# Second parts of weights kept in DRAM: own buffers for the work done ahead, and one unread matmul inside a norm's last sums

## The chip, the cores and the metric

The kernel runs on one core of a Trainium2 chip. The metric is the device time of one execution in microseconds. TensorE (PE) multiplies, VectorE (DVE) and ScalarE (ACT) do elementwise work, GpSimd (POOL) helps them, and SyncE (SP) issues most DMA transfers.

## The reference

One inference step of a decoder with two layers, for 256 prompt tokens and 8 x 4 sample tokens, T = 288 in all, width 2048. Each sub-layer stands between two RMS norms. The even layer mixes tokens by causal pooling and retention, the odd layer by a gating MLP and a convolution of 31 taps over 1024 channels; each layer ends with a dense MLP of 8192 hidden units.

```python
def _rms(x, g):
    y = xf * lax.rsqrt(jnp.mean(xf * xf, axis=-1, keepdims=True) + EPS)
...
for each layer:
    x = x + _rms(mixer(_rms(x, g0) @ w_in) @ w_out, g1)
    x = x + _rms(square(relu(_rms(x, g2) @ w_up)) @ w_down, g3)
```

## The kernel before

**Tiles and passes.** Activations lie transposed, 16 tiles of 128 channels by 288 tokens. Weights are float32; the kernel splits each weight into a hi part in TensorE's rounded float32 type (`whi`, a copy on ScalarE) and the rest (`wlo` = raw - whi, on VectorE), and the activations likewise (`xhi`, `xlo`, or `hidhi`, `hidlo`). Each product is three passes: hi by hi, lo by hi, hi by lo.

**Subs and groups.** The unit of weights is a sub: 256 rows by 512 columns, 512 KB, 24 matmuls. A group (`Grp`) is the subs that fill the same four accumulators of 128 outputs; behind its last sub `evac` empties them. There are 720 subs in a fixed order: the even layer's input projection and mixers; its output projection; the first feed-forward network ("ffn0": four quarters q, each with four up and four down groups of 8 subs, here up0q0g1 or dn0q2g3); the odd layer's input projection (8 groups of 8 subs: ga0, ga1, ga2, v0, v1, ga3, u0, u1); its output projection (two halves of four groups of 4 subs, here oo00 to oo13); the second feed-forward network.

**The weight path.** For each place of the list `feed`, SP loads the raw weights into one of 4 buffers (`emit_dma`), ScalarE makes whi (`emit_hi`) and VectorE wlo (`emit_lo`). The pairs lie in a ring of 3 plus, in some stages, `more_ring(n)` further slots. `run` is the loop over subs; at the start of each it issues pending writes (`put_out`), feeds up to two places ahead (`some`), and then issues the sub's matmuls (`emit_mm`, L604). A load stands in SP's order behind the wait for its buffer.

**Jobs.** In ffn0 the feed holds 60 extra places of kind "job", at subs 1 and 5 of a group (`JOBS`). A job splits a sub of a later stage and writes both parts to DRAM (`hik`, `lok`, L534). When that sub's turn comes its kind is "kept": its parts are loaded from there (L517, two transfers) and not split. Kept are all of ga0, every other sub of the rest of the odd layer, and the first group of the second feed-forward network. A job takes a slot of the ring, as a sub does.

**Norms.** At the end of a sub-layer `last_sums` adds up the squares of the last four tiles on TensorE (L313); `boundary` then issues `keep_warm` (L369, matmuls of ones with a sum that nobody reads), spreads the result (L303) and normalises.

**The convolution** of the odd layer runs in the background of the w_in_odd and w_out_odd subs: some channel tiles on VectorE (`conv_all`, cacc), some on ScalarE and POOL (`conv_slow`, tap), the sample tokens on POOL and VectorE (prod). A tap is issued only when an engine's load, counted in the planner's own costs, is under a cap. `conv_out` ends it with a layer norm (L1347, L313, L303).

All of ScalarE's, VectorE's and POOL's instructions pass one helper, so they all have line L162.

Of the kernel before, what the change touches and what calls it, by code (L numbers as in the profile page):

```python
# [19 lines left out]
T = SEQ + NS  # L20
# [158 lines left out]
def build(tc, ctx, I, O, C):  # L179
# [230 lines left out]

    def last_tiles(src, m):

        if m < OWN:
            add_sq(accs[0], 12 + m, src)
            return
        s = tmp()
        A.activation(out=s, in_=src, func=AF.Square)
        P["own", m] = s
# [3 lines left out]
    def last_sums(i):  # L422

        if i == 0:
            sum_open()
            sum_part(accs[0], first=True)
            sum_part(P.pop(("own", 1)))
        elif i == 1:
            sum_part(P.pop(("own", 2)))
            sum_part(P.pop(("own", 3)), last=True)  # L430

# [42 lines left out]
    RAW, RING = 4, 3  # L474
    JOBS = (1, 5)
    raws, his = {}, {}
# [15 lines left out]
    def emit_dma(p):  # L492
        kind, i = feed[p]
        if kind == "kept":
            return
        g, s = subs[i]
        raw = wp.tile([128, 2, 512], F32, tag="raw", name="raw", bufs=RAW)
        r0, r1 = g.rows[2 * s], g.rows[2 * s + 1]
        assert r1 == r0 + 1 and ORDER[i] == (*g.w, r0, tuple(g.pieces))
        for k in range(0 if p else 2):  # L500
            SP.dma_start(out=raw[:, k, :], in_=I["wt"][i, :, k, :])
        if p:
            SP.dma_start(out=raw, in_=I["wt"][i])
        raws[p] = raw
# [7 lines left out]
    def emit_hi(p):  # L512
        kind, i = feed[p]
        hi, lo = parts[p] = ring_slot()
        if kind == "kept":
            for a, b in zip((hi, lo), kept[i]):
                SP.dma_start(out=f(a), in_=b)  # L517
        else:
            A.activation(out=hi, in_=raws[p], func=AF.Copy)
        if kind != "job":  # L520
            his[i] = hi, lo

    def emit_lo(p):
        kind, i = feed[p]
        hi, lo = parts.pop(p)
        if kind != "kept":
            V.tensor_tensor(out=lo, in0=raws.pop(p), in1=f(hi), op=SUB)
        if kind == "job":
            kept[i] = [dram.tile([128, 2, 512], F32, tag=f"{t}{i}", name=f"{t}k") for t in ("hi", "lo")]
            W["out"] = [(b, a) for a, b in zip((hi, lo), kept[i])]  # L530

# [4 lines left out]
    def plan():  # L536

        todo = []
        where = {}
        at = 0  # L540
        for gi, g in enumerate(groups):
            for s in range(g.nsub):
                subs.append((g, s))
                if g.ahead and g.ahead(s):
                    todo.append(at + s)
            where[gi] = at
            at += g.nsub
        slots = [where[gi] + s for gi, g in enumerate(groups) if g.jobs for s in g.jobs]
        assert len(slots) >= len(todo)
        slots = dict(zip(slots, todo))  # L550
        ahead = set(todo)
        for i in range(len(subs)):
            pos.append(len(feed))
            feed.append(("kept" if i in ahead else "sub", i))
            if i in slots:
                feed.append(("job", slots[i]))
        n = 0
        for kind, i in feed:
            nraw.append(n)
            n += kind != "kept"  # L560
        nraw.append(n)
# [19 lines left out]
    def some(n):  # L581

        return min(W["split"] + n - 1, pos[W["now"]] + RING + W["extra"] - 1)

# [65 lines left out]
    def run():  # L650
# [3 lines left out]
        for i, (g, s) in enumerate(subs):  # L654
# [29 lines left out]
            if last:  # L684
                if g.defer:
                    for m in range(4):
                        if g.keep:
                            g.keep(m, g.ps[m][:, :T])
                        else:
                            A.copy(out=y(m), in_=g.ps[m][:, :T])  # L690
                    def rest(g=g):
                        yield from finish_pre(g.ready)
                        for m in range(0 if g.keep else 4):
                            g.evac(m, y(m))
                        if g.fin:
# [24 lines left out]
    def to_ffn():  # L720
        if E["stack"]:
            E["stack"].close()
            E["stack"] = None
        else:
            Q["stack"].close()
            less_ring()
        more_ring(2)


    def ffn(layer, last):  # L730
        wu, wd = ("w_up", layer), ("w_down", layer)
        for q in range(4):
            for gm in range(4):
                def ev_up(m, ps, gm=gm):
                    k = gm * 4 + m
                    u = W["pool"].tile([128, T], F32, tag="u", name="u", bufs=8)
                    V.scalar_tensor_tensor(out=u, in0=ps, scalar=0.0, in1=rb, op0=ALU.max, op1=MUL)
# [7 lines left out]
                def st_up(q=q, gm=gm):  # L745
                    if gm == 0:
# [4 lines left out]
                                  start=st_up, kouter=first, defer=first, jobs=() if last or first else JOBS,  # L751
                                  ahead=(lambda s: True) if last and first else None))
            for gm in range(4):
                def ev_dn(m, ps, gm=gm, q=q):
# [5 lines left out]
                    if q == 3:  # L760
# [3 lines left out]
                        else:  # L764
                            last_tiles(y(k), m)

                def fin_dn(q=q, gm=gm):
                    if q == 3 and gm == 3:
                        for m in range(4):
# [6 lines left out]
                                  post=to_odd if q == 3 and gm == 1 and not last else None,  # L776
                                  jobs=() if last or (q == 3 and gm == 3) else JOBS))

# [330 lines left out]
    def even():  # L1109
# [35 lines left out]
        for gm in range(4):  # L1145
            def ev_o(m, ps, gm=gm):
# [5 lines left out]
                else:  # L1152
                    last_tiles(ps, m)
                V.tensor_scalar_mul(out=y(k), in0=ps, scalar1=gain(1, 0, k))
# [337 lines left out]
    def odd():  # L1492
# [9 lines left out]
        def ga(j):  # L1502
            def post_ga():
                if j == 1:
                    bg_drain(st_["setup"])
                if j == 0:
                    while "begun" not in Q:
# [8 lines left out]
                              start=odd_open if j == 0 else None, post=post_ga, kouter=j == 0, defer=j == 0,  # L1516
                              ahead=lambda s: j == 0 or s % 2 == 1))

        def vgrp(gm):
            def post_v():  # L1520
                if gm == 1:
# [4 lines left out]
                              lambda m, ps: ev_v_odd(m, ps, gm), start=start_v_odd if gm == 0 else None,  # L1526
                              post=post_v, ahead=lambda s: s % 2 == 1))

        def ugrp(gm):
            def post_u():  # L1530
                if gm == 1:
                    bg_drain(st_["gate"])

                    def tail():
                        while any(c in bgs or c in fills for c in st_["conv"]):
# [6 lines left out]
            groups.append(Grp(w, [(512 * gm, 512)], list(range(KT)), xs, lambda m, ps: ev_u(m, ps, gm),  # L1542
                              start=start_u if gm == 0 else None, post=post_u, ahead=lambda s: s % 2 == 1))

        for fn, i in ((ga, 0), (ga, 1), (ga, 2), (vgrp, 0), (vgrp, 1), (ga, 3), (ugrp, 0), (ugrp, 1)):
            fn(i)
        for half in range(2):
            for gm in range(4):
                def ev_o(m, ps, gm=gm, half=half):
# [5 lines left out]
                    else:  # L1555
# [4 lines left out]
                        else:  # L1560
                            last_tiles(y(k), m)

                def post_o(gm=gm, half=half):
                    if half == 0 and gm == 3:
                        for c in st_["conv"]:
# [12 lines left out]
                                  before={0: hold_ring} if half == 0 and gm == 3 else None,  # L1578
                                  ahead=lambda s: s % 2 == 1))

# [129 lines left out]
```

## Time and profile before

| | |
|---|---|
| median of 3 runs | 2472.33 us (2472.2 to 2473.88) |
| profiled execution | 2476.82 us, span 2475.1 us |
| busy, share of the span | PE 98%, DVE 55%, ACT 44%, POOL 10% |
| granted TensorE clock, mean | 0.988 |
| ffn0 from its first down group to its last sums (548.75 to 1234.19) | 685.44 us |
| odd layer, input projection (1268.30 to 1505.61) | 237.31 us |
| odd layer, output projection and norm (1505.61 to 1640.08) | 134.5 us |

The span runs from the first to the last instruction of the profiled execution, and its time has some microseconds around it. Windows are in microseconds from the start of the span. A busy share of 98% hides that the stages differ; the rows further down are therefore taken by stage. A granted clock of 1.00 is 2.4 GHz, the upper of two levels.

### The profile page before, as it was taken

The page shows a single profiled execution, that of the slowest core. Times are in us where ns is not written, and L with a number is a line of the kernel's source. Part 1 is how long each engine was busy: PE and PEld are TensorE (multiplying, and loading weights), DVE is VectorE, ACT ScalarE, POOL GpSimd, SP SyncE. Part 2 cuts the span into 40 slices and gives each one's busy share as a digit, 9 for nine tenths or more (in the row PEclk, how much of TensorE's full clock was granted, in tenths as well). Part 3 has the DMA queues.
Part 4 walks back from the last instruction along what each step waited for, and adds up shares of the span by engine and source line. Part 5 has one row for each costly group of instructions (what it writes and reads, how often), then busy time and mean ns, then how long its engine had stood idle before and what let it go on. Part 6 is the DMA issues. An engine that isn't in the chain of part 4 may idle for free.

```text
span 2475.1 us, 43388 instructions
## 1 busy us (share of the span) xinstructions
PE 2420.7 (98%) x17976; PEld 2386.2 (96%) x17976; DVE 1360.7 (55%) x1844; ACT 1090.6 (44%) x1567; POOL 251.9 (10%) x293
## 2 busy tenths in 40 slices
PE   9999999999999999999999999899999999999997
PEld 8899999999999999999999999899999999999997
DVE  5665564764455556555546976346434544544453
ACT  5343443554544455455434443435434434433442
POOL 0521111000000000000114750100000000000011
PEclk9999999999999999999999999999999999999998
DMA  7555464588888888888775656455555554545552
GB/s 253 164 185 181 159 206 160 181 280 296 289 289 297 279 295 290 294 288 293 261 254 211 246 200 219 179 196 190 168 164 168 163 169 161 172 162 170 165 166 92
DMA packets 146871, 529.35 MB, mean 214 GB/s; under 512 B 16809, under 2 KB 17849, under 8 KB 146649
## 3 DMA queue, kind: packets, MB, share of 16 engines
q1 hardware_dynamic: 142240, 511.81, 60.4%
q0 software_dynamic: 4288, 14.71, 1.8%
q8 instruction: 140, 2.29, 0.4%
q14 instruction: 59, 0.48, 0.1%
q10 hardware_dynamic: 144, 0.07, 0.0%
HBM read 453.68 MB, written 73.87 MB: 213 GB/s over the span
## 4 chain that ended last, share of the span: by engine, by line
PE 84%; DVE 6%; DMA 4%; ACT 3%; issue 2%; SPq 0%; POOL 0%; DVEq 0%; ACTq 0%; POOLq 0%
PE mm L604 81%; DVE wlo L162 2%; DVE cacc L162 2%; DMA raw<-in_wt 2%; DMA wlo<-lok 1%; ACT whi L162 1%; ACT tmp L162 1%; PE ms L313 1%; DMA lok<-wlo 1%; PE po L995 1%; DVE tmp L162 1%; PE ms L999 0%; DVE conv L162 0%; DVE yo L162 0%; PE ms L303 0%
## 5 line engine op out<-in xcount | busy, mean ns | idle before, releaser
L162 DVE TENSOR_TENSOR wlo<-raw,whi 128x1024 fp32r<-128x1024 f32 (+1 forms) x721 | 886.9, 1240 | 751.1 <-ACT whi L162 737.3
L162 ACT ACTIVATE whi<-raw 128x1024 fp32r<-128x1024 f32 (+1 forms) x721 | 755.1, 1057 | 1011.2 <-PE mm L604 892.1
L604 PE MATMUL mm<-xhi,wlo 128*128 128x288 f32 x3200 | 944.9, 297 | 11.3 <-DVE wlo L162 9.2
L604 PE MATMUL mm<-xhi,whi 128*128 128x288 f32 x3200 | 944.2, 297 | 10.3 <-DVE tmp L162 6.2
L604 PE MATMUL mm<-xlo,whi 128*128 128x288 f32 x3200 | 919.6, 296 | 0.0
L604 PE MATMUL mm<-hidhi,whi 128*128 128x288 f32 x2560 | 754.8, 296 | 6.8 <-ACT whi L162 3.2
L604 PE MATMUL mm<-hidhi,wlo 128*128 128x288 f32 x2560 | 757.6, 297 | 2.5 <-DMA wlo<-lok 1.7
L604 PE MATMUL mm<-hidlo,whi 128*128 128x288 f32 x2560 | 745.2, 296 | 0.0
L604 PEld LDWEIGHTS mm<-xhi,wlo 128*128 128x128 f32 x3200 | 605.4, 189 | 16.0 <-DVE wlo L162 13.2
L604 PEld LDWEIGHTS mm<-xhi,whi 128*128 128x128 f32 x3200 | 605.9, 189 | 13.3 <-issue 6.8
L604 PEld LDWEIGHTS mm<-xlo,whi 128*128 128x128 f32 x3200 | 595.8, 189 | 0.5 <-DVE xlo L162 0.5
L604 PEld LDWEIGHTS mm<-hidhi,whi 128*128 128x128 f32 x2560 | 485.3, 190 | 8.1 <-ACT whi L162 3.4
L604 PEld LDWEIGHTS mm<-hidhi,wlo 128*128 128x128 f32 x2560 | 485.4, 190 | 3.3 <-DMA wlo<-lok 2.1
L604 PEld LDWEIGHTS mm<-hidlo,whi 128*128 128x128 f32 x2560 | 480.3, 189 | 0.0
L162 POOL TENSOR_TENSOR acc<-acc,tmp 128x288 f32<-128x288 f32 x55 | 53.3, 970 | 1657.1 <-ACT tmp L162 1654.3
L162 DVE TENSOR_TENSOR y<-mm,y 128x288 f32<-128x288 f32 x112 | 50.9, 457 | 103.3 <-PE mm L604 103.3
L162 DVE SCALAR_TENSOR_TENSOR u<-mm,rb 128x288 f32<-128x288 f32 x120 | 54.3, 457 | 71.2 <-PE mm L604 71.2
L162 DVE SCALAR_TENSOR_TENSOR cacc<-gx,vecs,cacc 128x256 f32<-128x256 f32 x168 | 68.5, 478 | 0.0
L162 ACT ACTIVATE hidhi<-u 128x288 fp32r<-128x288 f32 x128 | 56.9, 445 | 4.1
L162 ACT ACTIVATE u<-u 128x288 f32<-128x288 f32 x128 | 55.3, 432 | 7.0 <-DVE u L162 6.9
L162 POOL TENSOR_TENSOR conv<-conv,tap 128x256 f32<-128x256 f32 x60 | 53.7, 895 | 13.6 <-ACT tap L162 10.0
L162 DVE TENSOR_TENSOR hidlo<-u,hidhi 128x288 fp32r<-128x288 f32 x128 | 49.7, 450 | 0.0
(180 smaller groups left out, 909.8 us busy)
## 6 DMA issues: line engine op xcount, KB each, us to landing
raw<-in_wt SPq DMA_DIRECT2D x719, 512.0 KB, 4.2
hik<-whi SPq DMA_DIRECT2D x60, 512.0 KB, 6.4
lok<-wlo SPq DMA_DIRECT2D x60, 512.0 KB, 7.1
whi<-hik SPq DMA_DIRECT2D x60, 512.0 KB, 4.4
wlo<-lok SPq DMA_DIRECT2D x60, 512.0 KB, 5.8
s0t<-in_state_ret POOLq DMA_DIRECT2D x24, 256.0 KB, 3.3
out<-s0t POOLq DMA_DIRECT2D x24, 256.0 KB, 3.4
out<-yo SPq DMA_DIRECT2D x8, 288.0 KB, 2.4
```

Source lines behind the costliest of these rows:

```text
L162: return call(*args, **kw)
L313: PE.matmul(P["sums"][:, t:t + 1], lhsT=a[:, c:c + 128], rhs=ones[:, 0:1], start=first and t == 0, stop=last and t == 2)
L604: PE.matmul(ps, lhsT=lhsT[:, k, c], rhs=rhs, start=s == 0 and k == 0 and which == 0, stop=s == g.nsub - 1 and k == 1 and which == 2)
L995: PE.matmul(po[gq:gq + 32, 0:256], lhsT=E["qdm"][:, hh, 32 * (b + i):32 * (b + i + 1)], rhs=s[:, i, :], start=False, stop=b >= 4, tile_pos ...
```

## The change

Jobs no longer use the ring. They have buffers of their own, `jhi` (one) and `jlo` (two), and stand at subs 3, 5 and 7. In ffn0 the ring has 3 + 1 slots in place of 3 + 2, and the tile `u` has 4 buffers there in place of 8. A kept sub has a kind: of "both", hi and lo are stored and loaded, as before (ga0 and the first group of the second feed-forward network); of "lo", only lo is stored, and the raw weights are loaded again so that ScalarE makes hi. "lo" are all subs of ga1 to u1. At the three norms behind ffn0, the odd output projection and the second feed-forward network, one `keep_warm` matmul stands between the sums of the third and of the last tile.

```diff
-    def last_tiles(src, m):
+    def last_tiles(src, m, rest):
+        P["rest"] = rest
...
             sum_part(P.pop(("own", 2)))
+            if P.pop("rest"):
+                keep_warm(1)
             sum_part(P.pop(("own", 3)), last=True)
...
-    JOBS = (1, 5)
+    JOBS = (3, 5, 7)
...
-        if kind == "kept":
+        if kind == "both":
             return
...
-        hi, lo = parts[p] = ring_slot()
-        if kind == "kept":
-            for a, b in zip((hi, lo), kept[i]):
-                SP.dma_start(out=f(a), in_=b)
+        if kind == "job":
+            parts[p] = [W["pool"].tile([128, 2, 512], F32R, tag=t, name=t, bufs=n) for t, n in (("jhi", 1), ("jlo", 2))]
+            A.activation(out=parts[p][0], in_=raws[p], func=AF.Copy)
+            return
+        hi, lo = parts[p] = his[i] = ring_slot()
+        if kind == "both":
+            SP.dma_start(out=f(hi), in_=kept[i][0])
         else:
             A.activation(out=hi, in_=raws[p], func=AF.Copy)
-        if kind != "job":
-            his[i] = hi, lo
+        if kind != "sub":
+            SP.dma_start(out=f(lo), in_=kept[i][-1])
...
         if kind == "job":
-            kept[i] = [dram.tile([128, 2, 512], F32, tag=f"{t}{i}", name=f"{t}k") for t in ("hi", "lo")]
-            W["out"] = [(b, a) for a, b in zip((hi, lo), kept[i])]
+            out = (hi, lo) if feed[pos[i]][0] == "both" else (lo,)
...
-        return min(W["split"] + n - 1, pos[W["now"]] + RING + W["extra"] - 1)
+        return min(W["split"] + n - 1, pos[min(W["now"] + RING + W["extra"], len(subs)) - 1])
...
                         yield from finish_pre(g.ready)
+                        flush()
...
-                                  ahead=(lambda s: True) if last and first else None))
+                                  ahead=(lambda s: "both") if last and first else None))
...
-                                  jobs=() if last or (q == 3 and gm == 3) else JOBS))
+                                  jobs=() if last or (q == 3 and gm > 0) else JOBS))
...
-                              ahead=lambda s: j == 0 or s % 2 == 1))
+                              ahead=lambda s: "both" if j == 0 else "lo"))
...
-                                  ahead=lambda s: s % 2 == 1))
+                                  ahead=lambda s: "lo" if half == 0 and s % 2 else None))
```

In the built order 72 subs are kept, not 80: 16 of "both" and 56 of "lo". The last line's condition is evaluated when `half` is already 1, so no sub of the odd output projection is kept; before, 16 of them were. VectorE's splits go from 721 to 719 (647 wlo and 72 jlo), ScalarE's from 721 to 775, raw loads from 719 to 775, loads of kept parts from 120 to 88, writes from 120 to 88, and TensorE has three matmuls more.

The first place is SP's order in the second and third groups of ffn0. Before, between up0q0g1 and up0q0g2 (raw is a load of weights, hik and lok are writes of a job's parts):

```order
L503 DMA raw_5336<-in_wt 128x1024
L503 DMA raw_5365<-in_wt 128x1024
L503 DMA raw_5374<-in_wt 128x1024
L534 DMA hik_5372<-whi_5367 128x1024
L534 DMA lok_5373<-wlo_5368 128x1024
L503 DMA raw_5406<-in_wt 128x1024
L503 DMA raw_5436<-in_wt 128x1024
L503 DMA raw_5466<-in_wt 128x1024
L503 DMA raw_5495<-in_wt 128x1024
```

In the changed kernel, in up0q0g2 (k0 and k1 are the writes of a job's hi and lo):

```order
L542 DMA k0_5341<-jhi_5332 128x1024
L542 DMA k1_5342<-jlo_5333 128x1024
L506 DMA raw_5376<-in_wt 128x1024
L506 DMA raw_5405<-in_wt 128x1024
L506 DMA raw_5414<-in_wt 128x1024
L542 DMA k0_5411<-jhi_5402 128x1024
L542 DMA k1_5412<-jlo_5403 128x1024
L506 DMA raw_5446<-in_wt 128x1024
```

Within a group there are now three raw loads from one pair of writes to the next, where there were five.

The second place is ScalarE's order at the same point of the program. Before (whi_5367 is a job's, the others are subs'):

```order
L162 ACTIVATE whi_5332<-raw_5186 128x1024
L162 ACTIVATE whi_5362<-raw_5195 128x1024
L162 ACTIVATE whi_5367<-raw_5272 128x1024
L162 ACTIVATE whi_5402<-raw_5294 128x1024
L162 ACTIVATE whi_5432<-raw_5336 128x1024
```

In the changed kernel (jhi is a job's, in the one buffer):

```order
L162 ACTIVATE whi_5294<-raw_5154 128x1024
L162 ACTIVATE jhi_5332<-raw_5163 128x1024
L162 ACTIVATE whi_5337<-raw_5197 128x1024
L162 ACTIVATE whi_5372<-raw_5272 128x1024
L162 ACTIVATE jhi_5402<-raw_5298 128x1024
L162 ACTIVATE whi_5407<-raw_5335 128x1024
```

jhi_5402 writes over jhi_5332, whose write to DRAM is k0_5341 in SP's order above, and whi_5407 of the next sub stands behind it.

The third place is SP's order in the odd layer's input projection, from ga0 on into ga1. Before:

```order
L517 DMA whi_13864<-hik_5942 128x1024
L517 DMA wlo_13865<-lok_5943 128x1024
L503 DMA raw_13898<-in_wt 128x1024
L517 DMA whi_13948<-hik_6072 128x1024
L517 DMA wlo_13949<-lok_6073 128x1024
L503 DMA raw_13956<-in_wt 128x1024
```

In the changed kernel:

```order
L523 DMA whi_13874<-k0_5705 128x1024
L527 DMA wlo_13875<-k1_5706 128x1024
L527 DMA wlo_13905<-k0_5775 128x1024
L506 DMA raw_13908<-in_wt 128x1024
L527 DMA wlo_13959<-k0_5929 128x1024
L506 DMA raw_13962<-in_wt 128x1024
```

Each sub of ga1 and behind now has two transfers and no wlo on VectorE. Two subs had three transfers before, and now have four.

## Rows read from the trace of the kernel before

**Rows 1.** Busy time by stage; behind it granted clock, DMA share, GB/s.
```profile
core 0 of [0], span 2475.1 us
core 0: us, PE busy (x) PEld busy (x) DVE busy (x) ACT busy (x) POOL busy (x), PEclk, DMA share, GB/s
464.75:548.75 84.00, 80.10 (x590) 79.16 (x589) 54.71 (x75) 50.78 (x80) 0.85 (x1) 0.98 0.79 273
548.75:1234.19 685.44, 685.44 (x5186) 685.44 (x5185) 380.47 (x410) 330.48 (x401) 7.55 (x7) 1.00 0.84 288
1234.19:1268.30 34.11, 33.10 (x235) 31.65 (x233) 13.53 (x20) 13.52 (x23) 8.16 (x10) 0.95 0.70 230
1268.30:1505.61 237.31, 222.80 (x1632) 219.44 (x1631) 181.86 (x359) 100.82 (x191) 110.72 (x118) 0.97 0.62 225
1505.61:1627.50 121.89, 114.81 (x800) 112.96 (x801) 44.18 (x81) 47.70 (x90) 10.82 (x14) 0.93 0.60 217
1627.50:1640.08 12.58, 12.06 (x67) 10.80 (x65) 3.55 (x9) 3.81 (x9) 1.41 (x2) 0.73 0.55 205
```

**Rows 2.** Waits of PE in the input projection of the odd layer.
```profile
PE mm L604 <- DVE tmp L162: 6.2, 3, 3.0
PE ms L1439 <- DVE mb L162: 2.9, 1, 2.9
PE mm L604 <- DMA wlo<-lok: 2.0, 2, 1.2
PE mm L604 <- DMA whi<-hik: 1.3, 1, 1.3
```

**Rows 3.** Waits of PE in the output projection of the odd layer.
```profile
PE mm L604 <- ACT whi L162: 3.2, 1, 3.2
PE mm L604 <- DVE tmp L162: 2.1, 1, 2.1
PE mm L604 <- DMA wlo<-lok: 1.7, 2, 1.2
PE mm L604 <- DVE wlo L162: 0.9, 1, 0.9
PE mm L604 <- DMA whi<-hik: 0.5, 1, 0.5
```

**Rows 4.** Timeline of PE after one such wait.
```profile
1355.66 0.37 PE L604 MATMUL mm<-xhi,whi 128*128 128x288 f32 x1 [2.96 <-DVE tmp L162]
...
1356.56 0.44 PE L604 MATMUL mm<-xhi,whi 128*128 128x288 f32 x1
```

**Rows 5.** Groups of VectorE in the input projection of the odd layer.
```profile
L162 DVE TENSOR_TENSOR wlo<-raw,whi 128x1024 fp32r<-128x1024 f32 x29 | 44.1, 1520 | 22.5 <-ACT whi L162 22.5
```

**Rows 6.** Groups on the page; DMA issues on the page, with us to landing.
```profile
L162 DVE TENSOR_TENSOR wlo<-raw,whi 128x1024 fp32r<-128x1024 f32 (+1 forms) x721 | 886.9, 1240 | 751.1 <-ACT whi L162 737.3
L162 ACT ACTIVATE whi<-raw 128x1024 fp32r<-128x1024 f32 (+1 forms) x721 | 755.1, 1057 | 1011.2 <-PE mm L604 892.1
...
hik<-whi SPq DMA_DIRECT2D x60, 512.0 KB, 6.4
```

**Rows 7.** Timelines of POOL and of VectorE about 1346 us.
```profile
1345.09 3.10 POOL L162 TENSOR_TENSOR prod<-gx,vecs 128x992 f32<-128x992 f32 x1
...
1346.15 3.12 DVE L162 TENSOR_TENSOR wlo<-raw,whi 128x1024 fp32r<-128x1024 f32 x1
```

**Rows 8.** Timeline of PE at the norm behind the first feed-forward network.
```profile
1262.93 0.83 PE L313 MATMUL ms<-cg,tmp 128*128 128x1 f32 x6 [0.52 <-ACT tmp L162]
1263.62 1.61 PE L369 MATMUL ms<-acc,cg 128*128 128x288 f32 x4
```

**Rows 9.** One step of the chain that ended last, 464 to 500 us.
```profile
483.14 0.33 SPq L503
```

**Rows 10.** The line that writes kept parts, from 1000 to 1060 us.
```profile
L534 SPq DMA_DIRECT2D hik<-whi x5: 426/426/562, 1002.3 to 1053.1; - x5
...
DMA to landing us min/median/max: 5.0/6.7/7.7
```

More of the change, by code (lines that the diff above doesn't have):

```diff
@@ L525, in emit_lo @@
         hi, lo = parts.pop(p)
-        if kind != "kept":
-            V.tensor_tensor(out=lo, in0=raws.pop(p), in1=f(hi), op=SUB)
+        raw = raws.pop(p, None)
+        if kind in ("sub", "job"):
+            V.tensor_tensor(out=lo, in0=raw, in1=f(hi), op=SUB)
         if kind == "job":
-            kept[i] = [dram.tile([128, 2, 512], F32, tag=f"{t}{i}", name=f"{t}k") for t in ("hi", "lo")]
-            W["out"] = [(b, a) for a, b in zip((hi, lo), kept[i])]
+            out = (hi, lo) if feed[pos[i]][0] == "both" else (lo,)
+            kept[i] = [dram.tile([128, 2, 512], F32, tag=f"k{n}{i}", name=f"k{n}") for n in range(len(out))]
+            W["out"] = list(zip(kept[i], out))
     def put_out():
@@ L536, in plan @@
     def plan():
-        todo = []
+        todo, kinds = [], {}
         where = {}
@@ L543, in plan @@
                 subs.append((g, s))
-                if g.ahead and g.ahead(s):
+                kind = g.ahead(s) if g.ahead else None
+                if kind:
                     todo.append(at + s)
+                    kinds[at + s] = kind
             where[gi] = at
@@ L550, in plan @@
         slots = dict(zip(slots, todo))
-        ahead = set(todo)
         for i in range(len(subs)):
             pos.append(len(feed))
-            feed.append(("kept" if i in ahead else "sub", i))
+            feed.append((kinds.get(i, "sub"), i))
             if i in slots:
@@ L559, in plan @@
             nraw.append(n)
-            n += kind != "kept"
+            n += kind != "both"
         nraw.append(n)
@@ L723, in to_ffn @@
             E["stack"] = None
+            more_ring(1)
         else:
@@ L726, in to_ffn @@
             less_ring()
-        more_ring(2)
+            more_ring(2)
     def ffn(layer, last):
@@ L735, in ev_up @@
                     k = gm * 4 + m
-                    u = W["pool"].tile([128, T], F32, tag="u", name="u", bufs=8)
+                    u = W["pool"].tile([128, T], F32, tag="u", name="u", bufs=8 if last else 4)
                     V.scalar_tensor_tensor(out=u, in0=ps, scalar=0.0, in1=rb, op0=ALU.max, op1=MUL)
@@ L764, in ev_dn @@
                         else:
-                            last_tiles(y(k), m)
+                            last_tiles(y(k), m, True)
                 def fin_dn(q=q, gm=gm):
@@ L1152, in ev_o @@
                 else:
-                    last_tiles(ps, m)
+                    last_tiles(ps, m, False)
                 V.tensor_scalar_mul(out=y(k), in0=ps, scalar1=gain(1, 0, k))
@@ L1526, in vgrp @@
                               lambda m, ps: ev_v_odd(m, ps, gm), start=start_v_odd if gm == 0 else None,
-                              post=post_v, ahead=lambda s: s % 2 == 1))
+                              post=post_v, ahead=lambda s: "lo"))
         def ugrp(gm):
@@ L1542, in ugrp @@
             groups.append(Grp(w, [(512 * gm, 512)], list(range(KT)), xs, lambda m, ps: ev_u(m, ps, gm),
-                              start=start_u if gm == 0 else None, post=post_u, ahead=lambda s: s % 2 == 1))
+                              start=start_u if gm == 0 else None, post=post_u, ahead=lambda s: "lo"))
         for fn, i in ((ga, 0), (ga, 1), (ga, 2), (vgrp, 0), (vgrp, 1), (ga, 3), (ugrp, 0), (ugrp, 1)):
@@ L1560, in ev_o @@
                         else:
-                            last_tiles(y(k), m)
+                            last_tiles(y(k), m, True)
                 def post_o(gm=gm, half=half):
```

## The prediction

> **What bounds the kernel now.** I read first the table of windows by stage [rows 1]. In the long feed-forward window 548.75 to 1234.19 TensorE is busy for the whole 685.44 us at granted clock 1.00. Its 5186 matmuls are 216 subs of 24, so one sub takes 685.44 / 216 = 3.17 us. That stage is at its floor and can only be made slower. The odd layer is not: its input projection has 64 subs (203 us at 3.17) and takes 237.31 us, and its output projection has 32 subs (101 us) and takes 121.89 + 12.58 = 134.5 us. So 34 and 33 us lie above the floor there, part of it matmuls of the mixers and norms that stay whatever happens. TensorE sat idle for 237.31 - 222.80 = 14.5 us of the first, and a granted clock of 0.97 gives up 0.03 x 237 = 7 us more. In the second it is 7.1 us idle and 0.07 x 122 = 8.5 us of clock.
>
> What ended the idle time is in the views of waits. In the input projection [rows 2] it is VectorE by 9.1 us: 6.2 us in three waits for a tmp, which is the emptying of an accumulator, and 2.9 us for mb. DMA has only 3.3 us, in waits for kept parts. In the output projection [rows 3] it is the splitting itself, whi 3.2 and wlo 0.9 us, one late emptying of 2.1 us left over from the stage before, and 2.2 us of loads of kept parts. An idle stretch costs twice: after the 2.96 us wait at 1355.66 matmuls of the same kind go from 0.37 and 0.30 us to 0.44 us [rows 4], spaced at the lower of the two clock levels, 1.2 GHz, until the clock is granted in full again.
>
> VectorE is the late engine because it still splits 28 subs and runs the taps of the convolution. Its wlo instructions take 44.1 us of this stage, at 1520 ns each [rows 5] against 1240 ns over the whole program [rows 6]. The excess comes from single long ones: the wlo at 1346.15 took 3.12 us, and a POOL multiplication stood from 1345.09 to 1348.19 [rows 7]. The Trainium skill (SBUF — State Buffer, section "SBUF: two separate sides") describes it: a VectorE instruction with two SBUF inputs and a GpSimd one take a shared port pair in turns, each for its whole length. The row agrees. By it the wlos leave this lock and the two-input adds of the emptyings stay.
>
> **The change, part by part.** *Fewer splits in the input projection.* 28 of the 29 wlo instructions go; 28 whi on ScalarE come, which is busy 100.82 of 237 us [rows 1] and at 1.06 us each [rows 6] goes to 130; it hides them. Each of the 56 subs now loads a raw and a wlo, 1 MB per 3.17 us or 331 GB/s, where the stage moved 225 GB/s. 44.1 us less of VectorE in a stage with 181.86 us of it should take away its 9.1 us of waits, and with them the share of the lost clock that they caused, 7 x 9.1 / 12.4 = 5 us: together -14 us. Below, if the convolution, paced by a load meter, fills the freed time and is late at the same places, -4; above, all idle time and all lost clock, -21.
>
> *The tail of the convolution.* It is spread over more of the time before, and its layer norm is now seven subs earlier on TensorE, in oo00 instead of oo02. So the rush that ends at the start of the second half (3.2 + 0.9 us of splitting), the 2.1 us emptying and the 2.2 us for kept loads, of which the output projection has none now, should go: 8.4 us. Only two or three of the stage's clock losses follow from these; taken with a small part of them and with the 16 more splits per engine hidden under an engine that is busy 44 of 122 us, -9. Bounds: -3 (only the kept loads and one wait) and -13 (half of the 8.5 us too). I count here that the diff says 80 subs and the built order has 72: the condition for half 0 of the output projection is read when `half` is already 1, so none of its subs is kept.
>
> *The matmul at the norms.* It stands between the third tile's sums and the last's, where TensorE waits 0.52 us for ScalarE [rows 8]. Four recorded passes take 1.61 us, so one matmul of two passes takes about 0.7 us at full clock. It may end 0.2 us late, or keep the clock up for the spread behind it. Three places: -1 in sum, bounds -3 and +1.
>
> *The jobs.* This is the cost. A job that stores both parts (16 of 72) writes hi and lo to DRAM from its own buffers, and the hi has one buffer. So the next job's ScalarE copy waits until that write has landed, and in ScalarE's order the next sub's whi stands right behind the waiting copy (the second order table): everything TensorE needs next is held up. From one copy to the next write's issue: the copy 1.06, its lo and the next sub's lo on VectorE 2 x 1.24, and SP's issue of the raw load that stands ahead, 0.33 us [rows 9]: 3.9 us. The landing comes on top: hi writes 6.4 us over the run [rows 6], and 5.0 to 7.7 us (median 6.7) for the writes of five jobs about 1000 us [rows 10]. So 3.9 + 6.4 = 10.3 us per job, while the places in the groups leave two subs, 6.34 us, within a group and four, 12.7 us, across groups. A whi runs about three subs, 9.5 us, ahead of its use, some 8.1 us after its own time and its small waits; lateness up to there is free.
> First run (eight such jobs from the second group of the feed-forward on, and the plain job behind them): 8 x 10.3 = 82.4 us, allowed 6 x 6.34 + 2 x 12.7 = 63.4; 82.4 - 63.4 - 8.1 = +11 us. Before, that window had 84.00 us with 80.10 busy, moving 273 GB/s, so landings there will not be shorter. Second run (eight near the third quarter's end): 7 x 10.3 = 72.1, allowed 5 x 6.34 + 2 x 12.7 = 57.1; +7 us. Each brings about 0.5 us of clock: +1. With landings of 5.0 us the first run needs 71.2 against 71.5 allowed with the free lateness, and costs nothing; with 7.7 us it is +21 and the second +16. The jobs that store a lo alone have two buffers for it and wait on VectorE only; a group of eight subs then has eleven raws and three writes, as many transfers as before (ten raws and four writes from two jobs). What covers them is VectorE's free time, busy 380 of 685 us [rows 1]. At nothing; without that cover each late split would cost its 1.24 us.
>
> *Small pieces.* One wlo now stands inside the chain of the norm between the even layer and the feed-forward: +1 (0 to 1.24). Half the buffers for u, and an earlier flush of late instructions: at nothing, since these instructions run a whole group ahead of their reuse; if not, a wait of under 1 us per group would show in the stage that is now at 1.00.
>
> **The sum.** -14 - 9 - 1 + 11 + 7 + 1 + 1 = -4 us. The profiled execution took 2476.82 us with a span of 2475.1, which is 4.5 us above the median of the runs, 2472.33. So 2472.8 us by the profile's measure, 2468 by the median's. A measurement can tell about 0.2%, 5 us, from no change: the forecast lies just inside that.
>
> **The rivals.**
> *A, the writes land in time.* Only the gains are left: -24 + 1 for the norm's wlo = -23 us, 2449 us. For it: the shortest landing of 5.0 us suffices, stalls of TensorE make the queues emptier, and the cover may be more than 8.1 us. Against: the medians, 6.4 and 6.7 us [rows 6, 10]. The Trainium skill (DMA: Bandwidth & Descriptors, section "Anatomy of one DMA") gives 2.0 us plus bytes / 436 GB/s, for another path of issue; I estimate 3.2 us for 512 KB from it. By that the cycle is 7.1 us, and the chain costs nothing. The measured 6.4 us decides against it here.
> *B, the single buffer costs more than the odd layer gives.* This one ends on the other side. Eight jobs write 1 MB each while three raws per job are loaded too: in a group eleven raws and six writes, 17 x 0.524 MB in 25.4 us or 351 GB/s, where 288 GB/s moved at a DMA share of 0.84 [rows 1], which is at most 343 GB/s at a share of 1. If the landings therefore take 7.7 us, the runs cost +21 and +16, and the sum is +15: 2487 us. It decides from landings of about 6.7 us on, where the two runs cost +13 and +9 and the sum is zero.
> *C, the input projection becomes bound by its loads.* 331 GB/s is near the 343. Every sub late by a tenth would give 56 x 0.3 = +17 us and eat the gain: about 2485 us. Against: at the stage's start eight kept subs ask for two loads each now, and DMA waits there are 3.3 us in all [rows 2].
> *D, the change does less than it says.* As for the eight subs of the output projection, this is sure and in the sum; more of it, with the odd layer's waits returning at other places, gives -10 + 20 = +10, 2482 us, and lies with C in the chances.
>
> **Chances and range.** Mixed, as forecast (sum from -12 to +4): 0.48. A: 0.22. B: 0.19. C or D: 0.11. Faster by over 0.2%: all of A and 0.22 of the forecast's, 0.44. Within: 0.25 of the forecast's and 0.03 of C and D, 0.28. Slower: the rest, 0.28. The forecast's own range is 2460 to 2476. The whole range reaches to A and nearly to B: 2448 to 2486.
>
> **What would show it.** Right: in the profile after, ScalarE's jhi waiting for DMA in two groups of places, with TensorE waiting for whi behind it, about 11 us before the first down groups begin and 7 us near the end of the third quarter; the input projection near 223 us without waits for tmp; no wait for whi at the start of the second half of the output projection. Wrong: no jhi wait that reaches TensorE (A), DMA waits for wlo<-k all over the input projection (C), or tmp waits of the old size there (D).

## The result, and the profile after

The changed kernel takes 2494.5 us (median of 4 runs, 2493.33 to 2499.51) against 2473.06 us before: a ratio of 1.0091, with a 95% interval of 1.0073 to 1.0108. It is slower by 0.9%, 21 us; the forecast was 2468 us, 5 us less than before, with a range up to 2486. The profiled execution has a span of 2492.3 us, 17.2 us more than before, at a granted clock of 0.986 in place of 0.988. (It is 17 and not 21 because the profiled execution of the kernel before, 2476.82 us, was itself 4 us over its median.) The profile counts 721 splits on VectorE (649 wlo and 72 jlo) and 777 on ScalarE (705 whi and 72 jhi), two more on each than the counts given with the change.

The span is taken apart by the start of each stage's first matmul on TensorE. "Forecast" is the term of the prediction's sum.

| stage, first matmul to first matmul | before, us | after, us | change | forecast |
|---|---|---|---|---|
| start to ffn0's first up group | 437.11 | 439.59 | +2.5 | 0 |
| that group (norm, up0q0g0) | 27.64 | 28.76 | +1.1 | +1 |
| up0q0g1 to dn0q0g1 (first run of jobs of both parts) | 109.39 | 130.53 | +21.1 | +11.5 |
| dn0q0g1 to dn0q2g2 (jobs of lo alone) | 431.57 | 431.57 | 0.0 | 0 |
| dn0q2g2 to up0q3g2 (second run) | 101.55 | 114.28 | +12.7 | +7.5 |
| up0q3g2 to dn0q3g3 | 126.93 | 126.94 | 0.0 | 0 |
| dn0q3g3, norm, to ga0 | 34.11 | 32.46 | -1.7 | -0.3 |
| input projection, ga0 to oo00 | 237.31 | 219.43 | -17.9 | -14 |
| output projection, oo00 to oo11 | 86.99 | 88.14 | +1.2 | -9 |
| oo11 to the next up group, with the norm | 47.48 | 45.15 | -2.3 | -0.3 |

From there to the end the two differ by 0.4 us. The first row is not put down to the change: 1.6 us of it arise in the first two subs, where the order of instructions is the same, and 0.9 us at the norm in front of ffn0, which lasts 9.7 to 10.9 us in the profiles of the experiments; there that group starts anywhere from 437.7 to 440.5 us. Two rows cost what the gain of the odd layer cannot pay, and one row of that gain is missing.

The same windows in the profile after, with the columns of [rows 1], busy time by engine and behind it the granted clock, DMA share and GB/s; the first is the first run of jobs, the second lies in the second run, then the input projection (before in [rows 1]) and the output projection up to oo11:

```profile
468.35:598.88 130.53, 113.24 (x783) 110.33 (x782) 73.00 (x94) 66.12 (x99) 1.76 (x1) 0.92 0.75 254
1077.00:1124.00 47.00, 39.63 (x268) 38.15 (x268) 21.22 (x24) 19.95 (x25) 0.00 (x0) 0.93 0.81 282
1304.13:1523.56 219.43, 216.05 (x1631) 213.30 (x1631) 154.98 (x349) 129.02 (x220) 95.33 (x120) 1.00 0.86 308
1523.56:1611.70 88.14, 78.03 (x539) 77.10 (x538) 39.50 (x60) 44.16 (x76) 2.45 (x3) 0.88 0.39 128
```

Two of these stretches, cut at the same subs, in the profile before:

```profile
464.75:574.14 109.39, 105.49 (x782) 104.55 (x781) 69.76 (x91) 63.81 (x96) 0.85 (x1) 0.98 0.81 280
1505.61:1592.60 86.99, 79.91 (x537) 78.06 (x537) 34.71 (x67) 34.40 (x66) 2.48 (x3) 0.90 0.53 190
```

In the first run TensorE is idle for 130.53 - 113.24 = 17.3 us, where it was 3.9 us: 13.4 us more. The granted clock of 0.92 takes 0.08 x 130.53 = 10.4 us, where 0.98 took 2.2: 8.2 us more. The two add up to about the 21.1 us of the table. In the second run TensorE is idle for 8.0 us over the whole stretch, where it was never idle; the row shown has 7.4 of them and 0.07 x 47 = 3.3 us of clock. That is 11.3 of the 12.7 us. The input projection has 3.4 us idle and a clock of 1.00, before 14.5 us and 0.97. DMA moves 308 GB/s there at a share of 0.86 and TensorE does not wait for it much (below).

TensorE's waits in the first run: waiting instruction, releaser, us in total, times, longest:

```profile
PE ms L303 <- POOL sm L162: 7.7, 1, 7.7
PE mm L613 <- ACT whi L162: 4.8, 2, 2.6
PE mm L613 <- DVE wlo L162: 4.1, 5, 1.1
PE mm L613 <- DVE u L162: 0.6, 1, 0.6
```

The whi and wlo are what a late jhi holds up. The largest single wait is another: L303, the spread of the second norm, waits for a POOL step. The POOL step waited for VectorE's scalar instruction, which stood in VectorE's order behind a job's jlo and a wlo, and the jlo had waited 5.13 us for its jhi. VectorE's and POOL's timelines there:

```profile
495.72 1.23 DVE L162 TENSOR_TENSOR jlo<-raw,jhi 128x1024 fp32r<-128x1024 f32 x1 [5.13 <-ACT jhi L162]
496.87 1.22 DVE L162 TENSOR_TENSOR wlo<-raw,whi 128x1024 fp32r<-128x1024 f32 x1
498.00 0.15 DVE L162 TENSOR_SCALAR sm<-ms 128x3 f32<-128x3 f32 x1
498.23 1.76 POOL L162 TENSOR_TENSOR sm<-sm,cg 128x3 f32<-128x3 f32 x1 [62.04 <-DVE sm L162]
```

The chain that ended last, through two of the jobs (start, us, what; steps of under 0.2 us and the waits named issue are left out):

```profile
518.98 6.21 DMA k<-jhi
...
525.27 1.06 ACT jhi L162
...
527.50 1.23 DVE wlo L162
...
528.74 0.33 SPq L506
...
529.12 6.48 DMA k<-jhi
...
535.70 1.07 ACT jhi L162
```

From one jhi to the next it is 10.43 us: the copy, the next sub's wlo behind the job's own, SP's issue of the raw load that stands ahead (0.33 us), and 6.48 us until the written hi has landed. This is the cycle of 10.3 us that was forecast, and it has two subs, 6.34 us, of room.

What the clock adds shows in TensorE's timeline at the end of such a wait:

```profile
571.83 0.61 PE L613 MATMUL mm<-hidhi,wlo 128*128 128x288 f32 x1 [1.05 <-DVE wlo L162]
572.24 0.44 PE L613 MATMUL mm<-hidlo,whi 128*128 128x288 f32 x1
...
575.34 0.29 PE L613 MATMUL mm<-hidlo,whi 128*128 128x288 f32 x1
```

Until 575 us the same matmuls take 0.44 us, afterwards 0.29. So after a wait of 1.05 us, which itself followed one of 2.63 us for the same sub's whi, three microseconds ran at 1.2 GHz; the granted clock from 571.83 to 575.18 is 0.50. Each of the four largest groups of waits of this run has such a stretch at its end or behind it. The Trainium skill (TensorE: Matmul & The Clock Gate, Part 1) says that the slow clock is the default and that activity releases it. The rows agree: it is a row of matmuls without a gap that goes from 0.44 to 0.29 us.

TensorE's waits in the input projection after, and the largest one in the output projection:

```profile
PE mm L613 <- DMA wlo<-k: 2.3, 2, 1.4
PE ms L1450 <- DVE mb L162: 0.5, 1, 0.5
```

```profile
PE mm L613 <- ACT y L162: 8.8, 1, 8.8
```

The 9.1 us of waits for VectorE in [rows 2] are down to 0.5 us (mb). In the output projection one wait of 8.8 us, for an accumulator that ScalarE had not emptied, has come in the place of those of [rows 3]. ScalarE's timeline ahead of it:

```profile
1571.64 1.04 ACT L162 ACTIVATE whi<-raw 128x1024 fp32r<-128x1024 f32 x1
1575.09 0.63 ACT L162 ACTIVATE tmp<-tmp,vecs 128x288 f32<-128x288 f32 x1 [2.40 <-DVE tmp L162]
1575.74 0.44 ACT L162 ACTIVATE hidhi<-tmp 128x288 fp32r<-128x288 f32 x1
1576.09 0.61 ACT L162 ACTIVATE tmp<-tmp,vecs 128x288 f32<-128x288 f32 x1
1576.74 0.44 ACT L162 ACTIVATE hidhi<-tmp 128x288 fp32r<-128x288 f32 x1
1577.09 1.04 ACT L162 ACTIVATE whi<-raw 128x1024 fp32r<-128x1024 f32 x1
1580.52 0.63 ACT L162 ACTIVATE tmp<-tmp,vecs 128x288 f32<-128x288 f32 x1 [2.40 <-DVE tmp L162]
...
1583.47 1.28 ACT L162 COPY y<-mm 128x288 f32<-128x288 f32 x4
```

The round whi, tmp, hidhi, tmp, hidhi takes 5.43 us and a sub has 3.17. In each round the tmp waits 2.40 us for VectorE's tmp, which stands in VectorE's order behind that sub's wlo, which needs ScalarE's whi. After four rounds the four copies of y, which empty the accumulators (1583.47), are 9 us late.

In the kernel before the same loop came later and ran without a split between its rounds, 3.0 us each, and the whi that it held up followed in a row:

```profile
1573.59 0.63 ACT L162 ACTIVATE tmp<-tmp,vecs 128x288 f32<-128x288 f32 x1 [0.89 <-DVE tmp L162]
...
1576.59 0.63 ACT L162 ACTIVATE tmp<-tmp,vecs 128x288 f32<-128x288 f32 x1 [0.90 <-DVE tmp L162]
...
1578.58 2.94 ACT L162 ACTIVATE whi<-raw 128x1024 fp32r<-128x1024 f32 x3
```

### The profile page after: what moved, and what is told of

Same layout as the page of the kernel before. It is cut to its first block, busy times and chain, and to the rows that moved or that the text cites. A ratio compares the mean times of both kernels' runs of the same rounds, so it can differ in the third digit from the quotient of the medians.

```text
span 2492.3 us, 43540 instructions
## 1 busy us (share of the span) xinstructions
PE 2425.3 (97%) x17982; PEld 2387.8 (96%) x17982; DVE 1359.4 (55%) x1844; ACT 1145.1 (46%) x1623; POOL 239.9 (10%) x293
## 4 chain that ended last, share of the span: by engine, by line
PE 85%; DMA 4%; issue 4%; DVE 3%; ACT 3%; POOL 0%; SPq 0%; DVEq 0%; ACTq 0%; POOLq 0%
PE mm L613 82%; DMA k<-jhi 2%; DVE wlo L162 2%; DMA raw<-in_wt 1%; ACT whi L162 1%; ACT tmp L162 1%; DMA wlo<-k 1%; PE ms L313 1%; PE po L1006 1%; PE ms L1010 0%; ACT jhi L162 0%; DVE yo L162 0%; PE ms L303 0%; DVE hidlo L162 0%; POOL sm L162 0%
## 5 line engine op out<-in xcount | busy, mean ns | idle before, releaser
L162 ACT ACTIVATE whi<-raw 128x1024 fp32r<-128x1024 f32 (+1 forms) x705 | 741.1, 1057 | 927.0 <-PE mm L613 807.8
L162 DVE TENSOR_TENSOR wlo<-raw,whi 128x1024 fp32r<-128x1024 f32 (+1 forms) x649 | 794.6, 1231 | 662.6 <-ACT whi L162 661.9
L613 PE MATMUL mm<-hidhi,whi 128*128 128x288 f32 x2560 | 753.8, 295 | 11.5 <-ACT y L162 8.8
L162 DVE TENSOR_TENSOR jlo<-raw,jhi 128x1024 fp32r<-128x1024 f32 x72 | 88.0, 1222 | 89.5 <-ACT jhi L162 89.1
L162 ACT ACTIVATE jhi<-raw 128x1024 fp32r<-128x1024 f32 x72 | 76.0, 1055 | 103.8 <-DMA k<-jhi 81.3
L162 ACT ACTIVATE u<-u 128x288 f32<-128x288 f32 x128 | 55.3, 432 | 13.5 <-DVE u L162 13.4
```

Of the source, the lines that this page charges most:

```text
L162: return call(*args, **kw)
L613: PE.matmul(ps, lhsT=lhsT[:, k, c], rhs=rhs, start=s == 0 and k == 0 and which == 0, stop=s == g.nsub - 1 and k == 1 and which == 2)
```

## The experiments

Each kernel is the changed kernel with one edit or several. Stage times are taken as in the table above.

**Order of the jobs alone.**

```diff
+        both = [t for t in todo if kinds[t] == "both"]
+        lone = [t for t in todo if kinds[t] == "lo"]
+        todo = []
+        while both or lone:
+            todo += both[:1] + lone[:3]
+            both, lone = both[1:], lone[3:]
         slots = [where[gi] + s for gi, g in enumerate(groups) if g.jobs for s in g.jobs]
```

> The changed kernel with the same 72 jobs in the same 72 places and one change of order: of each four jobs one stores both parts and three store lo alone, instead of eight of both, 56 of lo and eight of both. Theory 1 (a job of both parts holds the one jhi until its write has landed, and only jobs in a row pile this up): a row of waits of 10.3 us against 6.34 us never builds up past one, so the two stretches lose their about 22 and 11 us, -33 us from the changed kernel, about 2461 us; single waits of jhi for DMA remain, none reaches TensorE for over 2 us. Rival (three jobs of any kind in a group, or the ring of 3 + 1, are too many for ScalarE, VectorE or DMA): the loss is spread over the feed-forward network or stays where it was; 2485 to 2495 us.

Measured: 2470.53 us, ratio 0.9997 (0.9986 to 1.0007) to the kernel before; 24 us less than the changed kernel. The first stretch takes 113.94 us in place of 130.53, and the second run's stretch 101.54, what it took before the change. But the groups between take 438.45 us in place of 431.57. There jhi now waits for its buffer too, 55.7 us in all between 575 and 1020 us, and TensorE has six short waits, 3.5 us together, for VectorE's u, wlo and y. That the held jhi is behind these is not shown; with two buffers the same order costs 0.7 us there (432.49 and 433.21 us in the last two kernels below). Theory 1 holds for the two runs; the shortfall of 9 us against the expected time lies in these 6.9 us and the 4.5 us that are left in the first stretch.

**Two buffers for jhi.**

```diff
-... for t, n in (("jhi", 1), ("jlo", 2))]
+... for t, n in (("jhi", 2), ("jlo", 2))]
```

> The changed kernel with two buffers for jhi in place of one; order and places of the jobs as in the changed kernel. Theory 1: with two buffers a job waits for the write before the last, 10.3 us against 12.7 or more, so the chain is gone: about -30 us, 2464 us. Rival 1b (the writes are slow because a group with three jobs of both parts moves 17 transfers, 351 GB/s, more than DMA can): the eight jobs in a row still take the time of the transfers, landings grow to 8 us and more, and at most 10 to 15 us come back, 2480 to 2485 us, while the spread order gets back all of it.

Measured: 2462.79 us, ratio 0.9967 (0.9957 to 0.9977): 32 us come back with one digit. The first stretch takes 110.48 us and the second run's 101.55; the groups between take 433.99 us, 2.4 more than before, and no run shows why. In the first run the jhi copies waited 41.5 us for their buffer in the changed kernel, in seven waits; with two buffers none waits for it. The window of the first run and its raw loads and hi writes (count, KB, us to landing) in this kernel:

```profile
467.42:577.90 110.48, 106.11 (x782) 104.67 (x782) 71.94 (x93) 65.12 (x95) 0.85 (x1) 0.98 0.81 296
```

```profile
raw<-in_wt SPq DMA_DIRECT2D x44, 512.0 KB, 5.8
...
k<-jhi SPq DMA_DIRECT2D x8, 512.0 KB, 6.8
```

In the changed kernel the same writes stand so:

```profile
k<-jhi SPq DMA_DIRECT2D x8, 512.0 KB, 6.5
```

With two buffers DMA moves 296 GB/s there, more than the 254 of the changed kernel, the writes take 6.8 us to land, more than the 6.5 there, and the loss is gone. So rival B's road, slow transfers in groups of 17, is out: what cost the time was that one buffer is held for a landing.

**The later start.** The first run's jobs begin one group later, past the norm.

```diff
-jobs=() if last or first else JOBS,
+jobs=() if last or (q == 0 and gm < 2) else JOBS,
```

> The changed kernel with no jobs in the second group of the feed-forward network, so that the first run of eight jobs of both parts begins one group later, behind the scalar step of the norm whose spread TensorE waited 7.7 us for; one buffer for jhi, the jobs otherwise in the same pattern. What is looked at is the stretch from the second up group to the second group of the first down quarter and the eight subs behind it: 109.4 us before, 130.5 changed. Theory 5 (the waits add to 10.3 us a job and are free up to 8 us, as predicted, but in the first run they met the norm, whose step stands in VectorE's order behind a job's lo and has no such reserve): without that meeting the run costs what was predicted, 11 us and about 1 of clock, in place of 21. Rival (a row of jobs of both parts costs 21 us wherever it begins, for example since landings or the reserve were misjudged): 19 to 23 us again, spread over the group ends.

Measured (one run): 2498.07 us. The norm's wait is gone, and the loss is still there: from up0q0g1 to dn0q2g2 560.90 us against 540.96 before the change, +19.9 us, where the changed kernel has +21.1. TensorE's waits in this stretch, and two of its jhi on ScalarE:

```profile
PE mm L613 <- ACT whi L162: 10.5, 4, 3.1
PE mm L613 <- DVE wlo L162: 5.8, 6, 1.1
```

```profile
516.28 1.06 ACT L162 ACTIVATE jhi<-raw 128x1024 fp32r<-128x1024 f32 x1 [9.17 <-DMA k<-jhi]
527.78 1.06 ACT L162 ACTIVATE jhi<-raw 128x1024 fp32r<-128x1024 f32 x1 [8.55 <-DMA k<-jhi]
```

The 16.3 us of waits are now for whi and wlo alone. Theory 5 falls, as far as one run can show it: the norm was only the place where the lateness of the first jobs came out, and one group later the run costs about as much.

**The bound condition**, 80 kept subs.

```diff
-... ahead=lambda s: "lo" if half == 0 and s % 2 else None
+... ahead=lambda s, half=half: "lo" if half == 0 and s % 2 else None
```

> The changed kernel with the condition of the output projection bound when it is written, so that subs 1 and 3 of the four groups of half 0 are kept with their lo: 80 kept subs. Theory 2 (the 8.8 us wait of TensorE for y at the end of oo02 comes from ScalarE and VectorE waiting for one another once per sub: whi, wlo, tmp, tmp on ScalarE, 5.4 us a round against 3.17): with eight fewer wlo the round is shorter in half of the subs, the wait falls below 4 us and with its clock about 7 us go, 2487 us. Rival (ScalarE's own work is too much there): the wait stays at 8 to 9 us, 2494 us; if the eight more jobs cost something in the feed-forward network, above that.

Measured: 2488.42 us, ratio 1.0066 (1.0041 to 1.0091). oo00 to oo10 takes 67.25 us in place of 75.42, and the wait for y 3.9 us in place of 8.8, as theory 2 has it.

**A pair of tiles scaled one step earlier.** In conv_out VectorE's multiplication by rl, now in place, is issued a step before ScalarE's use.

```diff
+        def scaled(k):
+            V.tensor_tensor(out=cv[:, k, :], in0=cv[:, k, :], in1=rl, op=MUL)
+
+        scaled(0)
+        scaled(1)
         for k in range(8):
-            t, s = tmp(), tmp()
-            V.tensor_tensor(out=t, in0=cv[:, k, :], in1=rl, op=MUL)
-            A.activation(out=s, in_=t, func=AF.Silu, scale=vec("cv_ln_g", k), bias=vec("cv_ln_b", k))
+            s = tmp()
+            A.activation(out=s, in_=cv[:, k, :], func=AF.Silu, scale=vec("cv_ln_g", k), bias=vec("cv_ln_b", k))
...
             if k % 2 == 1:
+                for n in (k + 1, k + 2):
+                    if n < 8:
+                        scaled(n)
```

> The changed kernel with one move in the end of the convolution: VectorE scales a pair of tiles (conv times rl, in place) one step before ScalarE uses them, not in the same step; number and kind of instructions are the same. Theory 2 (ScalarE and VectorE wait for one another): ScalarE's round falls from 5.4 us to its own work, whi 1.04 and four activations of 2.1 us, 3.2 us; the 8.8 us wait for y at the end of oo02 falls below 2 us, and with its clock about 10 us go: 2484 us. Rival (ScalarE or VectorE has too much work there): the wait stays, 2494 us.

Measured: 2487.79 us, ratio 1.0056 (1.0041 to 1.0071). oo02 to oo10 takes 26.98 us in place of 36.76, and the wait for y is down to this:

```profile
PE mm L613 <- ACT y L162: 1.3, 1, 1.3
```

The same kinds and numbers of instructions in another order take nearly all of the wait away, so it was ScalarE and VectorE waiting for one another, and neither had too much work. (The edit also takes one tmp buffer fewer per tile, but no row above shows a wait for one.) With the bound condition's result, theory 2 holds.

**Half of the lo subs.** Only every other sub from ga1 to u1 is kept.

```diff
-... ahead=lambda s: "lo"))
+... ahead=lambda s: "lo" if s % 2 else None))
```

> The changed kernel with only every other sub of ga1 to u1 kept (28 of lo in place of 56), so that VectorE makes 28 wlo there again, as before, and ScalarE all whi. What is looked at is the input projection alone, from ga0 to oo00: 237.3 us before, 219.4 us changed. Theory 3 (VectorE's 44 us of splits are what made the accumulators empty late): back to 232 to 240 us, with waits for tmp of 5 us or more. Rival (the convolution, paced by a load meter, or ScalarE, or the clock decides, not these splits): 218 to 226 us.

Measured (one run): the input projection takes 238.47 us, with these waits of TensorE:

```profile
PE mm L613 <- DVE tmp L162: 6.3, 3, 3.7
PE ms L1450 <- DVE mb L162: 3.5, 1, 3.5
PE mm L613 <- DMA wlo<-k: 3.0, 2, 2.2
```

That is the time and the waits of before [rows 2], at the same kind of places. Theory 3 holds: the 28 wlo on VectorE were the price. The whole run took 2510.08 us; its second run of jobs lies elsewhere and costs 10.6 us there.

This run also bears on the output projection. No sub of it is kept here either, so the 16 more splits per engine are there, but the end of the convolution is late again as before. The rush at oo10 is back (oo10 to oo11 19.99 us, 12.72 in the changed kernel, 22.74 before), the wait for y is not there, and oo00 to oo11 takes 83.66 us, less than the 86.99 before:

```profile
1544.99:1628.65 83.66, 75.77 (x537) 74.92 (x537) 48.17 (x80) 44.45 (x75) 1.68 (x2) 0.92 0.38 126
```

**No matmul at the norms.**

```diff
-            if P.pop("rest"):
-                keep_warm(1)
+            P.pop("rest")
```

> The changed kernel without the three matmuls at the norms. What is looked at is the two norms from dn0q3g3 to ga0 (34.1 us before, 32.5 changed) and from oo13 to up1q0g0 (22.1 and 19.8 us). Theory 4 (the matmul keeps the clock up through the end of the sums and the spread): both return to the times before, +1.7 and +2.3 us. Rival (the norms gained from the order of the splits about them, or from chance): both stay within 0.5 us of the changed kernel's.

Measured (one run, 2498.8 us): dn0q3g3 to ga0 33.59 us (32.46 with the matmul, 34.11 before), oo13 to up1q0g0 19.77 us (19.76 and 22.10). The second gain is there without the matmul. With the matmul the first norm took 34.00 us in the kernel with two buffers and 34.16 with the bound condition added, and the second one 22.27 in the kernel with the earlier scaling. What goes with the times is whether the clock fell there: in the thirteen traces the first norm takes 32.5 us where the granted clock stayed up and 33.6 to 35.0 us where it fell, and with the matmul it fell in four of eleven. Neither theory is shown: whether the matmul does anything stays open, and if it does, it is 1 to 2 us in some executions.

**Versions put together.** The spread order with the bound condition:

> Both edits, the spread order of the jobs and the 80 kept subs. By theories 1 and 2 the two add up: -33 and -7 us from the changed kernel, about 2454 us, which is faster than the kernel before by 19 us. By the rivals of both it is that of the changed kernel, 2494 us.

Measured: 2459.32 us, ratio 0.9949 (0.9934 to 0.9964), 5 us short of what was expected; the spread order alone had fallen short by 9. Two buffers with the bound condition:

> Two buffers for jhi and the bound condition (80 kept subs) together. If the parts of the odd layer and of the jobs are independent: 2462.8 us of two buffers alone, less the 6.1 us that the bound condition gave on the changed kernel, 2456.7 us; the stages oo00 to oo10 take 67 us as with the condition alone, the two stretches of the first feed-forward network as with two buffers alone. Rival (eight more jobs of lo do not fit beside the eight of both parts that they push towards the end of the network): 2462 us or more.

Measured: 2453.7 us, ratio 0.9920 (0.9903 to 0.9936): the two parts add up. With the earlier scaling as well:

> Two buffers for jhi, the bound condition and the move in the end of the convolution together: the version that the runs so far point to. The stretch from oo02 to oo10 took 31.1 us with the first two and 27.0 with the move alone, so 4 us less than with the first two, 2449 to 2450 us, faster than the kernel before by about 1%. If the bound condition had already taken all that the move can give there, 2453 to 2454 us.

Measured: 2449.05 us, ratio 0.9910 (0.9894 to 0.9925); the profiled execution of this kernel was its slowest, 2457.65 us. And with the spread order on top:

> The same with the spread order of the jobs as well. With two buffers the chain is gone already (110.5 us against 109.4 before in the first stretch), so the order should add nothing by theory 1: within 2 us of the kernel without it. Should it be faster by 2 us or more, then jobs in a row cost something besides the buffer, such as the transfers; should it be slower, the copies of jobs that wait among the down groups of the first quarter, where ScalarE empties accumulators, cost TensorE (the spread order with one buffer lost 6.9 us there).

Measured: 2447.26 us, ratio 0.9892 (0.9877 to 0.9907), the fastest of all, 26 us under the kernel before. Its intervals and those of the version without the spread order overlap, so the order adds nothing that these runs can tell.

## Why the prediction was wrong

Between the forecast of -4 us and the +17 of the profile lie 21 us. By the table the two runs of jobs make 15 of them (9.6 and 5.2) and the output projection 10; the first row adds 2.5, and the input projection and the norms give 7 back.

**The jobs.** The cycle was right, 10.43 us measured against 10.3, and so was its landing, 6.1 to 7.0 us (median 6.5) against 6.4. The waits that it makes for TensorE were nearly right: 13.4 us more idle time against 11 in the first run, 8.0 us against 7 in the second. The step that failed is "Each brings about 0.5 us of clock: +1". It measured 8.2 us in the first run and 3.3 in the second, 11.5 in place of 1. The prediction had said itself that an idle stretch costs twice [rows 4], and then charged each run with half a microsecond in all. In the input projection before, 14.5 us of idle time went with 7 us of clock; by that share the 18 us of waits come with 9 us of clock, and the sum would have been +4 in place of -4. Where the other 2.4 us of idle time in the first run come from is open; the norm does not account for them, as the later start shows (one run).

**The output projection.** The step that failed is "with the 16 more splits per engine hidden under an engine that is busy 44 of 122 us, -9". The waits that were to go did go: whi at the second half's start, wlo, tmp and the kept parts have none left, and oo10 to oo11 takes 10 us less. But a new wait came. The prediction took the earlier end of the convolution for a gain alone and priced the splits by busy time. Before, the rounds of that end ran late and without a split between, 3.0 us each. Seven subs earlier they run one to a sub, each with a whi and, as no sub is kept now, a wlo in it, and came to 5.4 us. Busy time was the wrong cover: ScalarE is idle for half of that stretch and VectorE for more, but in turns, waiting for each other. That brought the 8.8 us wait and its clock: +1.2 in place of -9. The 16 more splits alone did not: with half of the lo subs they are there beside a late end of the convolution, and oo00 to oo11 costs 3.3 us less than before (one run). The bound condition and the earlier scaling, each alone, take most of it back or all: 79.97 and 75.21 us in place of 88.14, where the forecast was 78.

**The input projection.** Right in its mechanism and sign. -17.9 against -14, inside the bounds of -4 and -21: idle time fell by 11.1 us and the clock's loss of 7 us went altogether. With the 28 wlo back on VectorE the time was back (one run). The convolution did not fill the freed time at the same places. Rival C did not come: DMA waits are 2.3 us.

**Rival B** had the sign and nearly the time (2487 us). That was luck: its reason, landings of 7.7 us from transfers too dense, was not what happened. The hi writes landed in 6.1 to 7.0 us in the first run, with a median of 6.5, below the 6.7 us from which it was to decide. What it had in common with the result is the single buffer.

**Small pieces.** The group with one wlo more in the chain of the norm took 1.1 us longer, as said; no run took the wlo alone away, so its part is not shown. The jobs of lo alone cost nothing: 431.57 us before and after. The matmul at the norms is not shown to have done anything. That 72 subs are kept and not 80 was counted rightly, but its price was not worked out: 6 us by the bound condition.

## What to carry to other kernels

A staging buffer that is written to DRAM is busy until the write has landed; with one buffer, every engine instruction that stands behind its next use pays for the landing, so count buffers by landing time over the distance of uses, not by transfer rate. Price a wait on TensorE with the clock behind it: here 8 us of clock came with 13 us of waits. And before calling work hidden under an engine's idle time, look whether that idle time is a wait for the partner whose work is being added; where a loop is moved to an earlier place, look what it will share each round with there.

## What was not expected of the hardware

The hi writes of 512 KB took 6.8 us to land (median of eight) while DMA moved 296 GB/s, and 6.5 us at 254 GB/s: a third of a microsecond more in denser traffic, with single writes from 6.1 to 8.5 us. In the window of 296 GB/s raw loads of the same size landed in 5.8 us, a microsecond sooner. The Trainium skill (DMA: Bandwidth & Descriptors, section "Anatomy of one DMA"), on transfers issued from GpSimd, says that a transfer counts as done only when its last byte is confirmed in the target's memory and that HBM is the heaviest target. These writes were issued from SP, and the trace shows only the whole time, so what part of it the confirmation takes is not shown.
